# The second pair of column tiles of an input projection: eight plain products in place of seven products of a Strassen-Winograd scheme

## The chip, the cores and the metric

The kernel runs on one core of a Trainium2 chip. The metric is the device time of one execution in microseconds (us), lower is better. Engines are named as in the profile: PE is the matrix engine (PEld its weight loads), DVE the vector engine, ACT the scalar engine, POOL the GpSimd engine, SP the engine that issues most loads and stores. L85 is line 85 of the kernel before.

## What is computed

One step of a decoder layer for 1024 prompt rows and 64 sample rows, all in float32:

```python
h = rmsnorm(x, g_pre)
proj = h @ w_in                       # 1024 x 6656
p_in, p_gate, c_val, c_glu, c_gate, q, x_gate = slices of 512 columns
merge_logits = the other 3 x 1024 columns
a     = pool_mix(p_in) * silu(p_gate)
u     = c_val * sigmoid(c_glu)        # then a causal depthwise conv, width 31, layernorm, silu
bconv = cv * silu(c_gate)
cattn = attention(q, mem_kv(memory)) * silu(x_gate)
merged = sum_n sigmoid(merge_logits[n]) * (branch_n @ w_branch[n])
x_new = x + rmsnorm(merged @ w_out, g_post)
```

Outputs are x_new, the last rows of the two mixers' inputs, and the memory keys and values.

## The kernel before

**Products.** Each float32 operand is split into two float16 parts, high and low (`hilo`: ACT writes the high part, L75, and DVE the low one, L77 or L79; some low parts with no scale go to POOL). A product of two split operands takes three matmuls (`mm3`, L85, L88, L89); below, "a product" is one such matmul of 128 x 128 weights with 512 columns.

**Pairs.** The projection's columns are worked through in pairs of 128-column tiles. A pair's weights are a 2 x 2 block: a11, a12 (first tile, upper and lower 512 rows of the weight) and a21, a22 (second tile). The tokens are a 2 x 2 block too: B11, B21 (first 512 tokens, upper and lower features) and b12, B22 (second 512). `pair` makes the four result blocks with the seven products of Strassen-Winograd, 7 x 12 matmuls, from sums s1 to s4 of weight blocks and T1 to T4 of token blocks. s1 to s4 are made by ACT negating two blocks (L498) and four accumulating DMAs on POOL's queue (L499, L505 to L507). The T's are made once, in `startup`, and split into the big tile BO.

The first pair (sigmoid of c_glu, channels 0 to 255) is worked in `startup` by eight plain products, 8 x 12 matmuls (`first`): two tiles, two token halves, two feature halves. The second pair (c_val, `val_pair(0)`) is the first that goes through `pair`; its loads and two of its seven products are drawn into `startup` (`early`). Then follow the pairs of q, x_gate, and so on: 25 pairs after the first.

**Samples.** The 64 sample rows take 64-column matmuls in stage m5 of each pair (`mm_smp`), from a11, a12, a22 and a21. For these a21 is split (L75 on ACT, L79 on DVE), in `base0` or `prep5`.

**Order.** The stage loop at the file's end emits, for each stage, the loads 12 stages ahead, the weight sums 8 ahead, the splits 3 ahead, then the stage's matmuls, its evaluation, and a number of convolution taps and of side-job steps given by RATES. Side jobs are generators: `states` (the sample states), `mem_kv` (memory keys and values), attention heads, pooling, layer norm. A scheduler then reorders the emitted instructions on each engine; on the chip each engine runs its list in that order. Convolution taps (L712, L714) keep their program order.

**Startup.** x is loaded, its row norms found, the first 512 tokens turned by PE transposes (`flip`, L228), scaled and split (B11, B21). `second_half(k)` does the same for the second 512 tokens, feature tiles k and k+4: DVE L292 and L295 make the differences `tq` from which the T's come, and L79 splits b12, B22 and T1. T3 and T4 are two POOL subtractions for each k (L312, L313) and two splits.

Of the kernel before, what the change touches and what calls it, by code (L numbers as in the profile page):

```python
# [7 lines left out]
F32 = mybir.dt.float32  # L8
# [30 lines left out]
RATES = [(1.1, 2.2), (1, 1.4), (0.9, 1), (1, 1.2), (2.3, 1.4), (1.1, 1.8), (0.8, 0.9), (1.3, 0.2), (0.8, 1)]  # L39
# [7 lines left out]
def hybrid_layer_kernel(ctx, tc, i, o):  # L47
# [167 lines left out]
    BS = cst.tile([P, 2, KT, NS], F16, name="BS")  # L215
    g_pre = cst.tile([P, KT], F32, name="g_pre")
# [19 lines left out]
    def startup():  # L236
# [34 lines left out]
        xs_r = rstds([xs])  # L271
        mem["r"] = rstds(mems)
# [9 lines left out]
        first(0, 0, [lambda k: bo(B11, k), lambda k: bo(B21, k)])  # L282
# [7 lines left out]
        def second_half(k):  # L290
# [6 lines left out]
            hilo(tq[k][:, 0], *bo(T1, k), -1.0)  # L297

        second_half(0)
        yield  # L300
        first(1, 0, [lambda k: bo(B11, k), lambda k: bo(B21, k)])
        yield
        for k in range(1, 4):
            second_half(k)
            yield
        for k in range(4):
            hilo(tq[k][:, 1], *bo(T2, k), -1.0)
        for r in range(2):
            first(r, HALF, [lambda k: (b12[k // 2][:, 0, k % 2], b12[k // 2][:, 1, k % 2]), lambda k: bo(B22, k)])
            for k in (2 * r, 2 * r + 1):  # L310
                t3, t4 = half(), half()
                nc.gpsimd.tensor_tensor(t3, tq[k][:, 1], hx[k][:, 0], ALU.subtract)  # L312
                nc.gpsimd.tensor_tensor(t4, hx[k][:, 1], tq[k][:, 1], ALU.subtract)  # L313
# [12 lines left out]
            hilo(hs_, BS[:, 0].rearrange("p k n -> p (k n)"), BS[:, 1].rearrange("p k n -> p (k n)"))  # L326
# [9 lines left out]
    def mem_kv():  # L336
        memT = [Q([P, 2, KT // 2, NMEM], F16) for _ in range(2)]
# [103 lines left out]
    def mm_smp(out, w, kh, start, stop):  # L441
        mm3(out, [(w[:, 0, k, :], w[:, 1, k, :], BS[:, 0, 4 * kh + k, :], BS[:, 1, 4 * kh + k, :]) for k in range(4)], start, stop)

    early = {}

    def pair(c0, dest, block, smp, sc=1.0 / WS):


        v = {}
# [44 lines left out]
        def base0():  # L494
            spl("a21", lambda: A(1, 0))
# [75 lines left out]
        ahead = not stages  # L571
# [4 lines left out]
        if ahead:  # L576
            early.update(
                load=[*loads], first=lambda: (prep_a11(), m0(), e0()),
                second=lambda: (prep3(), m3()))
# [753 lines left out]
    for _ in start:  # L1333
        pass
# [68 lines left out]
```

## Time and profile before

| what | value |
|---|---|
| runs | 1017.92, 934.6, 937.97 us; median 937.97 |
| the profiled execution | 935.87 us, of which the span from first to last instruction is 933.8 us |
| mean granted PE clock | 0.97 |
| PE busy | 858.4 us (92%), 5765 matmuls |
| DVE busy | 741.3 us (79%), 1141 instructions |
| ACT, POOL busy | 452.8 us (48%), 359.3 us (38%) |
| memory traffic | read 62.37 MB, written 6.33 MB |

How to read it: a row of the timeline is "start, duration, engine, line, operation, out<-in, shape, xcount [idle time of the engine just before <- what ended it]". A row of the windows is "from:to length, then busy time and (xcount) of PE, PEld, DVE, ACT, POOL, then the granted PE clock, the share of the DMA engines in use and GB/s". Matmuls overlap in the pipeline: their start-to-start distance is their price, and a duration of 0.38 us is longer than that.

### The profile page before, as it was taken

What the parts mean: (1) busy time and instruction counts of PE and PEld (TensorE: products, weight loads), DVE (VectorE), ACT (ScalarE), POOL (GpSimd) and SP (SyncE); (2) the same over time, 40 slices, a digit from 0 to 9 for tenths busy, and PEclk for the clock granted to TensorE, in tenths of its full rate; (3) what the DMA queues carried; (4) which work ended last, traced back from release to release, by engine and by line L of the source; (5) the groups of instructions that cost most, each with busy time, mean ns of one, the idle gap of its engine ahead of it and who ended that gap; (6) DMA issues with size and microseconds to landing.
All of it is one profiled execution on the core that took longest, in us unless ns stands there. A gap on an engine that the chain in (4) does not pass through costs nothing.

```text
span 933.8 us, 15219 instructions
## 1 busy us (share of the span) xinstructions
PE 858.4 (92%) x5765; PEld 459.7 (49%) x5765; DVE 741.3 (79%) x1141; ACT 452.8 (48%) x964; POOL 359.3 (38%) x384
## 2 busy tenths in 40 slices
PE   5869999899999869999989989999999999968996
PEld 3325444554455435555444545555545555535532
DVE  4698599999968999999999696559565544699876
ACT  7767446564653613323345444346445443545542
POOL 1364152344243380311235664516364213285500
PEclk8889999999999988999999999999999999998998
DMA  8635742225556222334444345545554656310132
GB/s 296 160 62 157 205 107 57 58 68 136 126 191 159 91 39 79 70 79 93 97 97 102 73 102 116 121 97 105 123 122 101 138 131 216 85 57 24 69 124 90
DMA packets 99238, 103.23 MB, mean 111 GB/s; under 512 B 5231, under 2 KB 71781, under 8 KB 99149
## 3 DMA queue, kind: packets, MB, share of 16 engines
q1 hardware_dynamic: 82748, 68.24, 23.3%
q0 software_dynamic: 16416, 34.02, 20.4%
q8 instruction: 45, 0.74, 0.3%
q14 instruction: 29, 0.23, 0.1%
HBM read 62.37 MB, written 6.33 MB: 74 GB/s over the span
## 4 chain that ended last, share of the span: by engine, by line
PE 40%; DVE 20%; issue 3%; DMA 2%; ACT 1%; POOL 0%; DVEq 0%; ACTq 0%; POOLq 0%
PE pm L85 10%; PE pm L88 9%; PE pm L89 9%; DVE q L714 6%; PE pb L88 4%; PE pb L89 3%; PE pb L85 3%; DVE ws L79 3%; DVE ws L77 2%; DMA raw<-raw 2%; DVE BO L79 1%; DVE q L1151 1%; DVE q L466 1%; DVE q L1090 1%; DVE q L1082 1%
## 5 line engine op out<-in xcount | busy, mean ns | idle before, releaser
L85 PE MATMUL pm<-BO,ws 128*128 128x512 f16 x836 | 320.7, 385 | 18.6 <-DVE q L787 4.8
L88 PE MATMUL pm<-BO,ws 128*128 128x512 f16 x836 | 321.2, 384 | 2.2 <-DVE BO L79 1.6
L89 PE MATMUL pm<-BO,ws 128*128 128x512 f16 x836 | 320.3, 384 | 1.2 <-DVE ws L77 0.9
L79 DVE SCALAR_TENSOR_TENSOR ws<-raw,ws 128x512 f16<-128x512 f32 x228 | 194.2, 869 | 60.1 <-ACT ws L75 58.5
L88 PEld LDWEIGHTS <-ws 128*128 128x128 f16 x1548 | 149.1, 99 | 135.4 <-issue 29.9
L85 PEld LDWEIGHTS <-ws 128*128 128x128 f16 x1548 | 148.8, 99 | 126.1 <-issue 17.2
L89 PEld LDWEIGHTS <-ws 128*128 128x128 f16 x1548 | 149.2, 99 | 123.5 <-issue 8.2
L75 ACT ACTIVATE ws<-raw 128x512 f16<-128x512 f32 x228 | 138.1, 625 | 121.8 <-PE pm L89 50.4
L714 DVE SCALAR_TENSOR_TENSOR q<-q,cw,q 128x1024 f32<-128x1024 f32 x120 | 174.2, 1462 | 0.2
L85 PE MATMUL pb<-q,ws 128*128 128x364 f16 (+1 forms) x288 | 92.2, 323 | 13.2 <-ACT q L75 8.4
L88 PE MATMUL pb<-q,ws 128*128 128x364 f16 (+1 forms) x288 | 92.5, 321 | 0.0
L89 PE MATMUL pb<-q,ws 128*128 128x364 f16 (+1 forms) x288 | 92.3, 321 | 0.0
L499 POOL DMA_DIRECT2D raw<-raw x25 | 21.9, 876 | 157.6 <-ACT raw L498 133.3
L513 ACT ACTIVATE h<-pm 128x512 f32<-128x512 f32 x75 | 44.2, 590 | 63.5 <-PE pm L89 63.3
L1151 DVE SCALAR_TENSOR_TENSOR q<-pb,q 128x364 f32<-128x364 f32 (+1 forms) x72 | 37.2, 527 | 22.1 <-PE pb L89 20.4
L466 DVE SCALAR_TENSOR_TENSOR q<-pm,h 128x512 f32<-128x512 f32 x51 | 34.8, 683 | 23.1 <-PE pm L89 13.2
L75 ACT ACTIVATE q<-q 128x1024 f16<-128x1024 f32 (+2 forms) x37 | 35.7, 972 | 29.6 <-DVE q L863 15.5
L507 POOL DMA_DIRECT2D raw<-raw x25 | 23.4, 935 | 66.3 <-issue 16.8
L506 POOL DMA_DIRECT2D raw<-raw x25 | 21.7, 867 | 65.6 <-DMA raw<-raw 25.3
L77 POOL TENSOR_TENSOR q<-q,q 128x1024 f16<-128x1024 f32 (+1 forms) x17 | 32.5, 1921 | 30.2 <-ACT q L75 30.2
L498 ACT ACTIVATE raw<-raw 128x512 f32<-128x512 f32 x50 | 30.9, 625 | 26.4 <-DVE ws L79 26.2
L85 PE MATMUL pm<-BS,ws 128*128 128x64 f16 x416 | 43.7, 194 | 0.0
(242 smaller groups left out, 1311.9 us busy)
## 6 DMA issues: line engine op xcount, KB each, us to landing
raw<-in_w_in SPq DMA_DIRECT2D x104, 256.0 KB, 3.0
raw<-raw POOLq DMA_DIRECT2D x100, 256.0 KB, 3.2
q<-in_x_prompt SPq DMA_DIRECT2D x16, 512.0 KB, 9.4
q<-q POOLq DMA_DIRECT2D x14, 544.0 KB, 5.8
raw<-in_w_branch SPq DMA_DIRECT2D x24, 256.0 KB, 3.8
q<-in_w_mem_kv SPq DMA_DIRECT2D x8, 512.0 KB, 6.8
q<-in_cache_mem_k SPq DMA_DIRECT2D x8, 512.0 KB, 3.7
q<-in_cache_mem_v SPq DMA_DIRECT2D x8, 512.0 KB, 9.4
```

The costliest lines, as they stand in the source:

```text
L75: nc.scalar.activation(hi, src, AF.Copy, scale=scale)
L77: (eng or nc.vector).tensor_tensor(lo, src, hi, ALU.subtract)
L79: nc.vector.scalar_tensor_tensor(lo, src, scale, hi, ALU.mult, ALU.subtract)
L85: ins = nc.tensor.matmul(out, wh, xh, start=start and j == 0, stop=False, skip_group_check=partial)
L88: nc.tensor.matmul(out, wh, xl, start=False, stop=False, skip_group_check=partial)
L89: nc.tensor.matmul(out, wl, xh, start=False, stop=stop and j == n - 1, skip_group_check=partial)
L466: nc.vector.scalar_tensor_tensor(dst, ps, sc, base, ALU.mult, ALU.add)
L498: nc.scalar.activation(A(1, kh), A(1, kh), AF.Copy, scale=-1.0)
L507: nc.gpsimd.dma_start(out=A(0, 1), in_=A(0, 0), accum_op=ALU.add)
L513: nc.scalar.activation(v[name], ps, AF.Copy, scale=sc)
L714: ins = nc.vector.scalar_tensor_tensor(acc, src, wj, acc, ALU.mult, ALU.add)
L1151: nc.vector.scalar_tensor_tensor(g, p, 1.0 / WS, g, ALU.mult, ALU.mult)
```

## The change

* The pair of c_val, channels 0 and 1 (`val_pair(0)`), is made by the new `plain_pair`: eight plain products (8 x 12 matmuls) instead of seven. Its four weight blocks are split in `startup` and no sums are made of them. The four products of the first token half are emitted ahead of most of `second_half`, and the remaining four are the pair's own first two stages; its samples are a third. A pair now stands for three stages at the head of the stage list instead of seven, and RATES gives each of them 4.8 side-job steps instead of 2.2.
* In every other pair, the second tile's samples are made from a22 and s1 instead of a22 and a21: the operand of s1 is the negated upper half of the samples (BSN), that of a22 the difference of the halves (BSD). s1 is minus the sum of a21 and a22, so the result is the same block. Both operands are split once, in `startup`. a21 is not split any more: one ACT and one DVE instruction of 128 x 512 less in each of 24 pairs. With the four splits that `plain_pair` doesn't need, 28 splits go on each of the two engines (228 to 200). POOL's queue loses four accumulating DMAs and three multiplications with the seven-product form of that pair.
* The splits of T1 are emitted after the second half's first product, those of T2, T3 and T4 after both.
* The loads of the states and of the memory are emitted in `startup`, after `second_half`, as the first step of their generators; the row norm of the samples goes behind them and that of the memory into `mem_kv`.

Core of the diff:

```diff
@@
-RATES = [(1.1, 2.2), (1, 1.4), (0.9, 1), (1, 1.2), (2.3, 1.4), (1.1, 1.8), (0.8, 0.9), (1.3, 0.2), (0.8, 1)]
+RATES = [(1.1, 4.8), (1, 1.4), (0.9, 1), (1, 1.2), (2.3, 1.4), (1.1, 1.8), (0.8, 0.9), (1.3, 0.2), (0.8, 1)]
@@
-        xs_r = rstds([xs])
-        mem["r"] = rstds(mems)
@@
-        first(0, 0, [lambda k: bo(B11, k), lambda k: bo(B21, k)])
+        first(0, 0, early["ops", 0])
@@
             hilo(p, *bo(B22, k), gk)
-            hilo(tq[k][:, 0], *bo(T1, k), -1.0)
@@
         second_half(0)
-        yield
-        first(1, 0, [lambda k: bo(B11, k), lambda k: bo(B21, k)])
-        yield
-        for k in range(1, 4):
-            second_half(k)
-            yield
-        for k in range(4):
-            hilo(tq[k][:, 1], *bo(T2, k), -1.0)
+        first(1, 0, early["ops", 0])
+        early["split"](0)
+        second_half(1)
+        early["first"](0)
+        early["split"](1)
+        second_half(2)
+        early["first"](1)
+        second_half(3)
+        for j in (states(), mem_kv()):
+            next(j)
+            jobs.append(j)
+        xs_r = rstds([xs])
         for r in range(2):
-            first(r, HALF, [lambda k: (b12[k // 2][:, 0, k % 2], b12[k // 2][:, 1, k % 2]), lambda k: bo(B22, k)])
-            for k in (2 * r, 2 * r + 1):
-                t3, t4 = half(), half()
-                nc.gpsimd.tensor_tensor(t3, tq[k][:, 1], hx[k][:, 0], ALU.subtract)
-                nc.gpsimd.tensor_tensor(t4, hx[k][:, 1], tq[k][:, 1], ALU.subtract)
-                hilo(t3, *bo(T3, k))
-                hilo(t4, *bo(T4, k), eng=nc.gpsimd)
+            first(r, HALF, early["ops", HALF])
             if r:
                 break
+            for k in range(4):
+                hilo(tq[k][:, 0], *bo(T1, k), -1.0)
...
+            hilo(hs_[:, :n], flat(BSN[:, 0]), flat(BSN[:, 1]), -1.0)
+            hd = half()[:, :n]
+            nc.vector.tensor_tensor(hd, hs_[:, n:], hs_[:, :n], ALU.subtract)
+            hilo(hd, flat(BSD[:, 0]), flat(BSD[:, 1]))
+        for k in range(4):
+            hilo(tq[k][:, 1], *bo(T2, k), -1.0)
+        for k in range(4):
+            t3, t4 = half(), half()
+            nc.gpsimd.tensor_tensor(t3, tq[k][:, 1], hx[k][:, 0], ALU.subtract)
+            nc.gpsimd.tensor_tensor(t4, hx[k][:, 1], tq[k][:, 1], ALU.subtract)
+            hilo(t3, *bo(T3, k))
+            hilo(t4, *bo(T4, k), eng=nc.gpsimd)
@@
+    def plain_pair(c0, block, smp):
+        raw, w = {}, {}
...
+        def split(r):
+            for kh in range(2):
+                w[r, kh] = new_ws()
+                hilo(raw[kh][:, r], w[r, kh][:, 0], w[r, kh][:, 1], WS)
+        def prod(r, t0):
+            p = pm()
+            for kh in range(2):
+                x = w[r, kh], early["ops", t0][kh]
+                mm3(p, [(x[0][:, 0, k, :], x[0][:, 1, k, :], *x[1](k)) for k in range(4)], kh == 0, kh == 1)
+            block(r, t0, p, 1.0 / WS)
...
+        early.update(load=[ldw(0), ldw(1)], split=split, first=lambda r: prod(r, 0))
+        for f in (lambda: prod(0, HALF), lambda: prod(1, HALF), samples):
+            stages.append([[], None, f, None, [], *rate, None])
@@
             spl("a22", lambda: A(1, 1))
-            spl("a21", lambda: A(1, 0))
@@
-            spl("a21", lambda: A(1, 0))
             spl("a22", lambda: A(1, 1))
@@
-            mm_smp(v["s"][:, NS : 2 * NS], v["w", "a22"], 1, True, False)
-            mm_smp(v["s"][:, NS : 2 * NS], v["w", "a21"], 0, False, True)
+            mm_smp(v["s"][:, NS : 2 * NS], v["w", "a22"], BSD, True, False)
+            mm_smp(v["s"][:, NS : 2 * NS], v["w", "s1"], BSN, False, True)
```

The scheduler gives every engine another order over about the first half of its list; after that the order is nearly the same, and the last eighth is as before on each. Three places, first as it was and then as it is. Lines are each version's own: L292, L295 are now L293, L296; L466 is L520, L712 to L729 are L757 to L774, L951 is L996, L1151 is L1196.

**DVE, the second token half in `startup`.** q_328 to q_331 before, and q_300 to q_303 now, are `tq` of k = 0 to 3; pb_332, pb_340 and pb_304, pb_312 are the PSUM banks of the turned tokens; q_326 and q_298 take b12.

```order
L292 SCALAR_TENSOR_TENSOR q_328<-pb_332,g_pre,q_136 128x512
L145 RECIPROCAL t_283<-t_279 128x2
L295 SCALAR_TENSOR_TENSOR q_328<-pb_340,g_pre,q_328 128x512
L150 TENSOR_TENSOR t_285<-t_283 128x2
L79 SCALAR_TENSOR_TENSOR q_326<-pb_332,g_pre,q_326 128x512
L151 TENSOR_TENSOR t_285<-t_285,t_281 128x2
L79 SCALAR_TENSOR_TENSOR BO<-q_328,BO 128x512
L152 TENSOR_SCALAR t_285<-t_285 128x2
L292 SCALAR_TENSOR_TENSOR q_329<-pb_394,g_pre,q_137 128x512
```

```order
L293 SCALAR_TENSOR_TENSOR q_300<-pb_304,g_pre,q_134 128x512
L296 SCALAR_TENSOR_TENSOR q_300<-pb_312,g_pre,q_300 128x512
L79 SCALAR_TENSOR_TENSOR q_298<-pb_304,g_pre,q_298 128x512
L79 SCALAR_TENSOR_TENSOR BO<-q_300,BO 128x512
L79 SCALAR_TENSOR_TENSOR ws_770<-raw_667,ws_770 128x512
L293 SCALAR_TENSOR_TENSOR q_301<-pb_352,g_pre,q_135 128x512
L79 SCALAR_TENSOR_TENSOR ws_881<-raw_688,ws_881 128x512
L79 SCALAR_TENSOR_TENSOR BO<-pb_312,g_pre,BO 128x512
```

The memory's row norm (t_279 to t_285) has left this place, and two weight splits of the q and x_gate pairs (ws_770, ws_881) stand in it. From the first scaling of the first token half (L264, now L265) to the last split of B22, the DVE list has 52 instructions of 128 x 512 and 4 of 128 x 1024 before, 51 and 2 now. The split `BO<-q` of T1 still stands inside, although it is emitted later.

**SP, the loads after the start.** raw_642, raw_645 before and raw_664, raw_667 now are the weights of the q pair; raw_724, raw_727 and raw_685, raw_688 those of the x_gate pair; raw_1104 is the pair after. A `raw` tile has four buffers.

```order
L195 DMA raw_642<-in_w_in 128x4x128 x2
L195 DMA raw_645<-in_w_in 128x4x128 x2
L405 DMA q_672<-in_state_conv 120x2x512
L408 DMA q_674<-in_state_pool 120x512
L410 DMA q_676<-in_pool_w 128x4x128
L195 DMA raw_724<-in_w_in 128x4x128 x2
L195 DMA raw_727<-in_w_in 128x4x128 x2
L344 DMA q_815<-in_w_mem_kv 128x2x512
```

```order
L196 DMA raw_664<-in_w_in 128x4x128 x2
L196 DMA raw_667<-in_w_in 128x4x128 x2
L196 DMA raw_685<-in_w_in 128x4x128 x2
L196 DMA raw_688<-in_w_in 128x4x128 x2
L422 DMA q_462<-in_state_conv 120x2x512
L425 DMA q_464<-in_state_pool 120x512
L427 DMA q_466<-in_pool_w 128x4x128
L166 DMA q_468<-in_mem_prompt 128x1024
L166 DMA q_470<-in_mem_prompt 128x1024
L196 DMA raw_1104<-in_w_in 128x4x128 x2
L361 DMA q_857<-in_w_mem_kv 128x2x512
```

The memory's rows (q_468, q_470), which stood right behind the sample rows, have moved to behind the states, and the first memory weights (q_815, now q_857) stand behind the first two loads of one pair more than before.

**DVE, at the end of the sample attention.** sxs is the attention's result for the samples, on which the last products of the first merge stages wait; q_3601 (now q_3575) and q_2565 (now q_2610) are convolution accumulators.

```order
L712 TENSOR_SCALAR q_3601<-q_2806,cw,parT 128x1024
L728 TENSOR_REDUCE v_3559<-q_3532 128x32
L728 TENSOR_REDUCE v_3605<-q_3562 128x32
L714 SCALAR_TENSOR_TENSOR q_3601<-q_2806,cw,q_3601 128x1024
L729 TENSOR_SCALAR q_1045<-v_3559,parT 128x32
L951 TENSOR_TENSOR sxs<-pb_2621,sxs 128x256
L729 TENSOR_SCALAR q_1045<-v_3605,parT 128x32
```

```order
L759 SCALAR_TENSOR_TENSOR q_2610<-q_443,cw,q_2610 128x1024
L773 TENSOR_REDUCE v_3530<-q_3486 128x32
L79 SCALAR_TENSOR_TENSOR ws_3804<-raw_3648,ws_3804 128x512
L773 TENSOR_REDUCE v_3559<-q_3533 128x32
L1196 SCALAR_TENSOR_TENSOR q_3232<-pb_3514,q_3232 128x364
L759 SCALAR_TENSOR_TENSOR q_2610<-q_443,cw,q_2610 128x1024
L996 TENSOR_TENSOR sxs<-pb_2568,sxs 128x256
L774 TENSOR_SCALAR q_1034<-v_3530,parT 128x32
```

sxs now stands ahead of the first tap L757 and of both L774, and behind two taps, one weight split and one evaluation.

More of the change, by code (lines that the diff above doesn't have):

```diff
@@ L215, in hybrid_layer_kernel @@
     BS = cst.tile([P, 2, KT, NS], F16, name="BS")
+    BSN = cst.tile([P, 2, KT // 2, NS], F16, name="BSN")
+    BSD = cst.tile([P, 2, KT // 2, NS], F16, name="BSD")
     g_pre = cst.tile([P, KT], F32, name="g_pre")
@@ L280, in first @@
             nc.scalar.activation(sg0[r][:, t0 : t0 + HALF], p, AF.Sigmoid, scale=1.0 / WS)
-        first(0, 0, [lambda k: bo(B11, k), lambda k: bo(B21, k)])
+        early["ops", 0] = [lambda k: bo(B11, k), lambda k: bo(B21, k)]
+        early["ops", HALF] = [lambda k: (b12[k // 2][:, 0, k % 2], b12[k // 2][:, 1, k % 2]), lambda k: bo(B22, k)]
+        first(0, 0, early["ops", 0])
         scale_x(xt[4:6], rs_[0], True)
@@ L336, in mem_kv @@
     def mem_kv():
+        mems = [load(i["mem_prompt"][0, t * P : (t + 1) * P, :], P) for t in range(2)]
+        yield
+        mem["r"] = rstds(mems, Q([P, D]))
         memT = [Q([P, 2, KT // 2, NMEM], F16) for _ in range(2)]
@@ L439, in mm_op, with mm_smp, ldw, f @@
         mm3(out, [(w[:, 0, k, :], w[:, 1, k, :], BO[:, n, 0, k, :], BO[:, n, 1, k, :]) for k in range(4)], start, stop, True, pinned)
-    def mm_smp(out, w, kh, start, stop):
-        mm3(out, [(w[:, 0, k, :], w[:, 1, k, :], BS[:, 0, 4 * kh + k, :], BS[:, 1, 4 * kh + k, :]) for k in range(4)], start, stop)
+    def mm_smp(out, w, x, start, stop):
+        mm3(out, [(w[:, 0, k, :], w[:, 1, k, :], x[:, 0, k, :], x[:, 1, k, :]) for k in range(4)], start, stop)
+    BS0, BS1 = BS[:, :, : KT // 2], BS[:, :, KT // 2 :]
     early = {}
+    def plain_pair(c0, block, smp):
+        raw, w = {}, {}
+        def ldw(kh):
+            def f():
+                raw[kh] = load_pair(kh, c0)
+            return f
+        def split(r):
[8 more added lines that the diff above has]
+            block(r, t0, p, 1.0 / WS)
+        def samples():
+            p = pm()
+            for r in range(2):
+                for kh, x in enumerate((BS0, BS1)):
+                    mm_smp(p[:, r * NS : (r + 1) * NS], w[r, kh], x, kh == 0, kh == 1)
+            for r in range(2):
+                smp(r, p[:, r * NS : (r + 1) * NS])
+        early.update(load=[ldw(0), ldw(1)], split=split, first=lambda r: prod(r, 0))
+        for f in (lambda: prod(0, HALF), lambda: prod(1, HALF), samples):
+            stages.append([[], None, f, None, [], *rate, None])
     def pair(c0, dest, block, smp, sc=1.0 / WS):
+        if not stages:
+            plain_pair(c0, block, smp)
+            return
         v = {}
@@ L471, in prep0 @@
         def prep0():
-            if not ahead:
-                prep_a11()
+            prep_a11()
         def prep1():
@@ L575, in pair @@
         loads = [ldw(0), ldw(1)]
[L576 to L579, printed above, removed]
-            loads, preps[3], mms[0], evs[0], mms[3] = [], None, None, None, None
         for j in range(7):
@@ L1323, in hybrid_layer_kernel @@
         stages[at + s][4].append(load_x(*tts))
-    start = startup()
     for f in early["load"]:
         f()
-    next(start)
-    next(start)
-    early["first"]()
-    next(start)
-    early["second"]()
-    for _ in start:
-        pass
+    startup()
     pps = pb()
```

18 lines of the change are left out of this document (8 added, 10 removed).

## Prediction

> **What bounds the kernel now.** I read the page's busy times first, then PE's windows, then the rows where PE waits.
>
> ```profile
> PE 858.4 (92%) x5765; PEld 459.7 (49%) x5765; DVE 741.3 (79%) x1141; ACT 452.8 (48%) x964; POOL 359.3 (38%) x384
> ```
>
> ```profile
> 0.00:40.00 40.00, 29.12 (x126) 16.23 (x127) 23.53 (x56) 28.55 (x53) 9.61 (x42) 0.87 0.79 251
> 40.00:70.00 30.00, 17.69 (x72) 7.62 (x71) 27.30 (x37) 21.86 (x36) 17.36 (x15) 0.83 0.35 68
> 70.00:130.00 60.00, 60.00 (x424) 31.97 (x422) 45.28 (x60) 35.29 (x67) 19.20 (x20) 1.00 0.57 160
> 130.00:310.00 180.00, 171.14 (x1250) 96.42 (x1249) 160.49 (x246) 97.75 (x216) 69.26 (x66) 1.00 0.44 110
> 310.00:355.00 45.00, 32.54 (x257) 17.89 (x255) 43.51 (x40) 16.10 (x32) 24.28 (x12) 0.85 0.26 67
> 355.00:450.00 95.00, 94.68 (x619) 51.47 (x617) 95.00 (x116) 34.27 (x64) 15.62 (x17) 1.00 0.39 86
> 450.00:560.00 110.00, 100.96 (x669) 50.01 (x667) 98.06 (x111) 50.23 (x99) 59.87 (x51) 0.98 0.41 93
> 560.00:815.00 255.00, 253.92 (x1714) 138.69 (x1713) 149.76 (x242) 118.26 (x231) 98.53 (x97) 1.00 0.54 124
> 815.00:850.00 35.00, 25.03 (x147) 12.96 (x146) 33.33 (x49) 15.97 (x45) 25.34 (x25) 0.90 0.17 53
> ```
>
> PE is the bound nearly everywhere: it is busy without a break from 70 to 130, from 355 to 450 and from 560 to 815 us. There a DVE instruction less is worth nothing, although DVE is full from 355 to 450. Time lies open where PE idles: in the startup (40 to 70: 12 us idle, at a clock of 0.83), at 310 to 355 (12 us, clock 0.85), at 450 to 560 (9 us) and in the tail, whose order the change leaves alone.
>
> The hole in the startup, on PE:
>
> ```profile
> 22.41 0.59 PE L88 MATMUL pm<-BO,ws 128*128 128x512 f16 x1 [0.63 <-DVE BO L77]
> 30.04 0.38 PE L88 MATMUL pm<-BO,ws 128*128 128x512 f16 x1
> 30.25 0.38 PE L89 MATMUL pm<-BO,ws 128*128 128x512 f16 x1
> 40.62 0.38 PE L89 MATMUL pm<-BO,ws 128*128 128x512 f16 x1
> 44.96 0.59 PE L85 MATMUL pm<-q,ws 128*128 128x512 f16 x1 [3.96 <-ACT q L75]
> 47.15 0.63 PE L89 MATMUL pm<-q,ws 128*128 128x512 f16 x1
> 47.57 0.63 PE L85 MATMUL pm<-q,ws 128*128 128x512 f16 x1
> 50.81 1.09 PE L228 MATMUL pb<-ident,q 128*128 128x128 f32 x4 [1.75 <-DVE BO L79]
> 58.80 0.59 PE L85 MATMUL pm<-q,ws 128*128 128x512 f16 x2 [2.03 <-ACT q L75]
> ```
>
> ```profile
> 41.00:68.00 27.00, 14.69 (x59) 6.32 (x58) 24.30 (x33) 19.13 (x33) 15.36 (x13) 0.81 0.35 68
> ```
>
> A product costs 0.21 us at full clock (30.04 to 30.25) and 0.42 at the clock granted after a wait (47.15 to 47.57). In 27 us PE runs 59 matmuls, at most 59 x 0.21 = 12.4 us of work. DVE is busy for 24.3 of these 27 us: it makes the splits of the second token half, which PE waits for directly or behind ACT. So the hole is DVE's.
>
> **The change part by part.**
>
> *Startup.* PE now has 24 + 24 products of the second pair that need the first token half alone, so it has work while DVE prepares the second half. What decides is when DVE finishes the last split of B22, because behind it PE has all operands of both pairs. These rows bound the run of DVE that leads there:
>
> ```profile
> 15.24 1.41 DVE L264 SCALAR_TENSOR_TENSOR q<-pb,g_pre,h 128x512 f32<-128x512 f32 x2 [0.57 <-ACT h L257]
> 71.42 0.74 DVE L79 SCALAR_TENSOR_TENSOR BO<-pb,g_pre,BO 128x512 f16<-128x512 f32 x1
> ```
>
> ```profile
> 15.00:72.00 57.00, 49.72 (x74) 0.82 0.51 126
> ```
>
> ```profile
> 46.28 3.01 DVE L152 TENSOR_SCALAR t<-t 128x2 f32<-128x2 f32 x1
> 54.38 0.74 DVE L79 SCALAR_TENSOR_TENSOR q<-pb,g_pre,q 128x512 f16<-128x512 f32 x1
> 55.04 2.32 DVE L79 SCALAR_TENSOR_TENSOR BO<-q,BO 128x512 f16<-128x512 f32 x1
> ```
>
> ```profile
> L312 POOL TENSOR_TENSOR h<-q,q 128x512 f32<-128x512 f32 x4 | 5.7, 1435 | 0.2
> L77 POOL TENSOR_TENSOR BO<-q,BO 128x512 f16<-128x512 f32 x4 | 5.7, 1442 | 18.7 <-ACT BO L75 18.7
> L77 POOL TENSOR_TENSOR BO<-h,BO 128x512 f16<-128x512 f32 x3 | 4.8, 1598 | 3.0 <-ACT BO L75 3.0
> L313 POOL TENSOR_TENSOR h<-q,q 128x512 f32<-128x512 f32 x3 | 4.6, 1528 | 0.6 <-DVE BO L77 0.6
> ```
>
>
> Before, it runs from 15.2 to 72.1: 52 instructions of 128 x 512, 4 of 128 x 1024 and 18 small ones. At their undisturbed 0.64 us each from start to start (0.66 from 54.38 to 55.04), 0.7 and 0.15 these would take 33.3 + 2.8 + 2.7 = 39 us. It was busy 49.7, so some 11 us are instructions that last longer than they need, such as 2.32 for a split of 0.7 or 3.01 for a tiny one, beside POOL's work; and 57 - 49.7 = 7 us are idle.
>
> Now the list has 51, 2 and 14: 32.6 + 1.4 + 2.1 = 36 us. That is hardly less, so the gain is mostly in what stands beside it. The last fence groups POOL's fourteen vector instructions from 19 to 71 us. Of these (four low parts of the first half, seven subtractions, three low parts of T4) eight can fall into the run: behind the first four subtractions POOL's next entry is a low part of T4, which waits for ACT's high part, and ACT has that behind all its splits of the second half. So lengthening is 8/14 of 11 = 6 us, and idle time, for weights still landing and for ACT's order, I leave at 5. DVE ends at 15.2 + 36 + 6 + 5 = 62. The ends: 51 with neither, 70 with all 18 us of both kept. By the first, PE itself would decide: to that point its list has 132 products and some 40 transposes from 22.4 us on, 132 x 0.21 = 27.7, ten at the slow clock 2.1 more, and 4 for the transposes (four take 1.09 at half clock): 57.
>
> From there PE's list holds 142 products, 96 of 64 columns and some 28 transposes until the memory keys' products end. Before, an almost equal stretch (137, 96 and 28) ran gapless:
>
> ```profile
> 68.17 0.38 PE L85 MATMUL pm<-BO,ws 128*128 128x512 f16 x1
> 103.15 0.38 PE L89 MATMUL pb<-q,q 128*128 128x512 f16 x1
> ```
>
> That is 35.2 us, so 36.3 now, ending at 98.3 instead of 103.4; and 20 products of the q pair more stand ahead of that point, worth 4.3. Startup net: 103.4 - 98.3 + 4.3 = **9.4 us won**, the 12 additional products (12 x 0.21 = 2.5) counted in. The ends: 14.4 won (PE's own 57) and 1.4 (70).
>
> *a21 never split.* 24 ACT and 24 DVE instructions less, 28 with the second pair's.
>
> ```profile
> L79 DVE SCALAR_TENSOR_TENSOR ws<-raw,ws 128x512 f16<-128x512 f32 x228 | 194.2, 869 | 60.1 <-ACT ws L75 58.5
> ```
>
> At 0.87 us that is 24 us of DVE, but most of it falls where PE is busy all the time. It pays only where DVE's list holds PE up:
>
> ```profile
> 335.76 4.34 DVE L712 TENSOR_SCALAR q<-q,cw,parT 128x1024 f32<-128x1024 f32 x1
> 343.41 5.00 DVE L729 TENSOR_SCALAR q<-v,parT 128x32 f32<-128x32 f32 x1
> 348.33 0.41 DVE L951 TENSOR_TENSOR sxs<-pb,sxs 128x256 f32<-128x256 f32 x1
> 349.08 0.76 PE L85 MATMUL pb<-q,ws 128*128 128x360 f16 x2 [8.36 <-ACT q L75]
> ```
>
> PE waits 8.4 us for the sample attention's result, which DVE reaches behind a tap of 4.34 us (L712) and a tiny L729 of 5.00. In the new order both stand behind it; one tap, one split and one evaluation more stand ahead, about 2.3 us. That would be 7 us; but most of the 9.3 is waiting beside POOL, which may hit another instruction as well. I take **4 won**, bounds 0 and 7. In 450 to 560 and in 130 to 310 PE idles 9 us each; two or three splits less there may win 2 or a new order lose 3: I take 0.
>
> *At nothing.* The sample operands BSN and BSD (three DVE, two ACT instructions, under 2 us) stand behind B22's last split, under PE's gapless stretch; without that cover they would cost their 2 us. Sample matmuls keep their number. s1's weights are now held until stage m5, a21's no longer: no more of the 13 buffers. The moved loads of states and memory rows are wanted only in that stretch too. Four accumulating DMAs less free POOL's queue while PE doesn't wait for them.
>
> *Sum.* 933.8 - 9.4 - 4 = 920.4 of span; with the 2.1 us by which the execution (935.87) exceeds its span 922.5. The median of the runs, 937.97, is 2.1 above that execution, so I say **923 us**.
>
> **A rule that speaks against it.** On the row of 2.32 us above bears what the Trainium skill says in "SBUF — State Buffer", section "SBUF: two separate sides": DVE and GpSimd share one port pair as an exclusive lock, and a DVE instruction with two SBUF inputs waits out a GpSimd instruction that reads SBUF. The trace agrees here: the split with one PSUM input took 0.74. By this rule the seven T splits `BO<-q` that still stand ahead of B22's last split can each be blocked, which would give rival 1.
>
> **The rivals.**
>
> 1. *The hole moves instead of closing.* Seven T splits stay in DVE's run; if POOL's work lengthens them as it did the one of 2.32 us, and the idle time stays, DVE ends at 70. Startup then wins 1.4, and nothing at 349: 935.9 - 1.4 = 934.5. For it: nearly equal counts, 52 and 51. Against it: POOL's list stops behind four subtractions.
>
> 2. *The memory's weights come late: slower.* Place: the first memory product on PE.
>
> ```profile
> 81.55 2.19 SPq L344 DMA_DIRECT2D q<-in_w_mem_kv  x4
> 92.15 0.59 PE L85 MATMUL pb<-q,q 128*128 128x512 f16 x2
> ```
>
> It starts 10.6 us after the load is issued. Now PE gets to it at about 62 + 25 = 87, so the load must be issued by 76; but on SP it stands behind raw_1104, which needs a buffer whose last split is DVE's 26th instruction behind B22's, some 14 us later, that is at 76, if the memory rows' norm, which also stands ahead there, isn't late. Each us after 76 is one of PE's. From 76 + 9.4 + 4 = 89 on, the kernel is slower; at 100 it would take 935.9 + 11 = 947. Against it: nothing ahead of that split waits for PE.
>
> 3. *The wait at 349 goes entirely, and DVE's relief also shortens 450 to 560*: startup 12, 7 there, 3 later: 935.9 - 22 = 914.
>
> 4. *It doesn't do what it says*: PE idles in the second half for want of ACT (40 to 70: 21.9 us busy of 30). The last split then comes no sooner than in rival 1, with the same time.
>
> **How the numbers follow.** A change of 2% (18.8 us, to 919.2) is about what a measurement of this kernel can tell. Chances: the forecast, 917 to 931, 0.6; rivals 1 and 4 together 0.2; rival 2 0.08; rival 3 0.12. The unknown costs give 935.9 - 14.4 - 9 = 912.5 to 935.9 - 1.4 + 3 = 937.5, and so the range is 912 to 938; it leaves out some 0.06 of rival 3 and 0.08 of rival 2. Faster by over 2%: rival 3 and a third of the lower half of the forecast, 0.22; slower by over 2%: half of rival 2, 0.04; within: 0.74.
>
> **What would show it.** Right: from 41 to 68 us PE's window holds over 100 matmuls instead of 59, at a clock above 0.9; DVE's last split `BO<-pb` ends near 62; the memory keys' products end near 98; the gap before the products on sxs is about 4 us instead of 8.4; `ws<-raw` on DVE is there 200 times; from 560 us on, shifted, the windows are as before. Wrong: a last split near 70; a gap of some us before the first memory product; or a startup that comes early and a loss of the same size at 130 to 310, where DVE is busy for 160 of 180 us.

## The result, and the profile after

The changed kernel takes 939.16 us (median of 17 runs), the one before, in 17 runs beside it, 934.60: a ratio of 1.0055, 95% interval 1.0041 to 1.0068. That is slower by half a per cent, where 923 was forecast. One run of each seventeen was far longer (1783.55 and 1017.92 us) and is left out of the ratio. The base was a little off too: the 935.87 us of the profiled execution, from which the forecast took its terms, is 1.3 us above the median of the seventeen.

The profiled execution took 941.47 us, its span 939.7. The page's busy times, and then five windows:

```profile
PE 860.9 (92%) x5777; PEld 460.6 (49%) x5777; DVE 722.8 (77%) x1116; ACT 433.4 (46%) x933; POOL 353.1 (38%) x377
```

```profile
41.00:68.00 27.00, 22.94 (x127) 11.42 (x126) 25.06 (x36) 17.64 (x32) 13.89 (x14) 0.87 0.48 110
70.00:130.00 60.00, 53.38 (x361) 28.67 (x360) 37.06 (x50) 29.65 (x56) 11.61 (x14) 0.94 0.52 143
130.00:310.00 180.00, 168.56 (x1201) 93.95 (x1200) 155.43 (x234) 92.17 (x209) 68.92 (x65) 0.98 0.42 109
310.00:355.00 45.00, 31.92 (x285) 18.15 (x281) 44.09 (x35) 17.97 (x34) 28.57 (x14) 0.91 0.25 60
355.00:450.00 95.00, 92.43 (x602) 50.04 (x600) 94.46 (x118) 32.31 (x62) 15.30 (x16) 0.97 0.37 84
```

The hole did close: 127 matmuls from 41 to 68 us where there were 59. But from 70 to 130 PE, gapless before, runs 361 instead of 424 at a clock of 0.94. What happened there stands in one row each of PE, ScalarE and SP:

```profile
87.22 1.12 PE L370 MATMUL pb<-ident,q 128*128 128x128 f32 x4 [5.99 <-ACT es L439]
107.19 0.38 PE L89 MATMUL pb<-q,q 128*128 128x512 f16 x1
```

```profile
74.75 1.17 ACT L433 ACTIVATE us<-pb 128x240 f32<-128x240 f32 x4
84.67 0.63 ACT L549 ACTIVATE raw<-raw 128x512 f32<-128x512 f32 x1 [8.75 <-DMA raw<-in_w_in]
85.20 0.82 ACT L75 ACTIVATE q<-pb,parT 128x256 f16<-128x256 f32 x2
86.21 0.47 ACT L75 ACTIVATE q<-pb,parT 128x256 f16<-128x256 f32 x1 [0.19 <-DVE q L79]
86.58 0.58 ACT L439 ACTIVATE es<-pb 128x480 f32<-128x480 f32 x1
```

```profile
80.58 0.93 SPq L196 DMA_DIRECT2D raw<-in_w_in  x2
81.61 0.96 SPq L361 DMA_DIRECT2D q<-in_w_mem_kv  x2
```

Read from below. SP issues the weights of the second attention pair (raw_1104) at 80.58, because only then is a raw buffer free. ScalarE's next entry is the sign change of exactly these weights (L549, in `base0`), and it waits 8.75 us for them. Behind it stand the splits of the turned memory rows and es, small instructions whose operands PE had made by 80.3 us, and PE waits for these: 5.99 us. From 80 to 90 us its granted clock is 0.72. The memory keys' products end at 107.6; before, at 103.5. VectorE waits for the same splits, 5.15 us until 85.69.

Why the buffer was free at 80.6 and not at 76, as the prediction had it, shows on VectorE:

```profile
58.02 0.73 DVE L79 SCALAR_TENSOR_TENSOR BO<-pb,g_pre,BO 128x512 f16<-128x512 f32 x1
69.35 1.20 DVE L151 TENSOR_TENSOR t<-t,t 128x2 f32<-128x2 f32 x1
72.94 2.28 DVE L356 TENSOR_SCALAR q<-q,t 128x1024 f32<-128x1024 f32 x2
78.14 2.40 DVE L79 SCALAR_TENSOR_TENSOR ws<-raw,ws 128x512 f16<-128x512 f32 x2
```

The last split of B22 ends at 58.8, not 72.2 (62 was forecast). The 26 instructions behind it then take 22 us instead of the 14 counted. In between stands the memory rows' norm, with five instructions on 2 elements of 1.0 to 1.2 us each (the sixth takes 0.15).

The second term of the sum, sxs, on VectorE, GpSimd and PE:

```profile
343.86 9.55 DVE L759 SCALAR_TENSOR_TENSOR q<-q,cw,q 128x1024 f32<-128x1024 f32 x1
353.33 0.41 DVE L996 TENSOR_TENSOR sxs<-pb,sxs 128x256 f32<-128x256 f32 x1
```

```profile
342.95 0.86 POOL L558 DMA_DIRECT2D raw<-raw  x1 [2.87 <-DVE ws L79]
343.52 8.80 POOL L770 TENSOR_TENSOR q<-us,cw 128x992 f32<-128x992 f32 x4
```

```profile
354.09 0.76 PE L85 MATMUL pb<-q,ws 128*128 128x360 f16 x2 [7.12 <-ACT q L75]
```

The tap that now stands right ahead of sxs takes 9.55 us where it needs 1.27. It begins 0.3 us after a train (several instructions of one engine, back to back) of four products of the convolution's samples on GpSimd, and ends 1.1 us after these are through, about its own running time. PE waits 7.12 us instead of 8.36, not 4.

### The profile page after: what moved, and what is told of

It is laid out like the page before. It is cut to its first block, busy times and chain, and to the rows that moved or that the text cites. A ratio compares the mean times of both kernels' runs of the same rounds, so it can differ in the third digit from the quotient of the medians.

```text
span 939.7 us, 15132 instructions
## 1 busy us (share of the span) xinstructions
PE 860.9 (92%) x5777; PEld 460.6 (49%) x5777; DVE 722.8 (77%) x1116; ACT 433.4 (46%) x933; POOL 353.1 (38%) x377
## 4 chain that ended last, share of the span: by engine, by line
PE 43%; DVE 31%; DMA 9%; issue 8%; ACT 6%; POOL 2%; SPq 1%; DVEq 0%; ACTq 0%; POOLq 0%
DVE q L759 12%; PE pm L85 10%; PE pm L88 10%; PE pm L89 10%; DVE ws L79 5%; DMA raw<-in_w_in 5%; PE pb L88 4%; PE pb L89 4%; PE pb L85 4%; DVE ws L77 3%; DVE BO L79 2%; DMA raw<-raw 1%; ACT ws L75 1%; DMA q<-q 1%; DVE q L1196 1%
## 5 line engine op out<-in xcount | busy, mean ns | idle before, releaser
L79 DVE SCALAR_TENSOR_TENSOR ws<-raw,ws 128x512 f16<-128x512 f32 x200 | 168.6, 861 | 41.6 <-ACT ws L75 40.5
L759 DVE SCALAR_TENSOR_TENSOR q<-q,cw,q 128x1024 f32<-128x1024 f32 x120 | 181.0, 1519 | 0.4
L75 ACT ACTIVATE ws<-raw 128x512 f16<-128x512 f32 x200 | 118.4, 624 | 87.7 <-PE pb L89 29.2
L549 ACT ACTIVATE raw<-raw 128x512 f32<-128x512 f32 x48 | 30.2, 628 | 85.7 <-DMA raw<-in_w_in 57.7
L550 POOL DMA_DIRECT2D raw<-raw x24 | 21.8, 907 | 126.8 <-ACT raw L549 120.1
L1196 DVE SCALAR_TENSOR_TENSOR q<-pb,q 128x364 f32<-128x364 f32 (+1 forms) x72 | 37.2, 528 | 26.1 <-PE pb L89 20.9
L520 DVE SCALAR_TENSOR_TENSOR q<-pm,h 128x512 f32<-128x512 f32 x48 | 32.7, 683 | 27.9 <-PE pm L89 18.2
L557 POOL DMA_DIRECT2D raw<-raw x24 | 20.8, 866 | 87.9 <-DVE ws L79 29.3
L77 POOL TENSOR_TENSOR q<-q,q 128x1024 f16<-128x1024 f32 (+1 forms) x17 | 35.4, 2088 | 39.8 <-ACT q L75 39.5
L558 POOL DMA_DIRECT2D raw<-raw x24 | 20.8, 866 | 73.3 <-DVE ws L79 43.5
L709 ACT ACTIVATE q<-q 128x512 f32<-128x512 f32 x36 | 22.6, 629 | 39.0 <-DVE q L520 38.7
```

The costliest lines, as they stand in the source:

```text
L75: nc.scalar.activation(hi, src, AF.Copy, scale=scale)
L77: (eng or nc.vector).tensor_tensor(lo, src, hi, ALU.subtract)
L79: nc.vector.scalar_tensor_tensor(lo, src, scale, hi, ALU.mult, ALU.subtract)
L520: nc.vector.scalar_tensor_tensor(dst, ps, sc, base, ALU.mult, ALU.add)
L549: nc.scalar.activation(A(1, kh), A(1, kh), AF.Copy, scale=-1.0)
L709: nc.scalar.activation(dst, src, AF.Sigmoid, scale=scale)
```

## The experiments

Theory A, from these rows: the startup's gain is lost to ScalarE's queue, and what the unsplit a21 should bring is eaten by VectorE waiting beside GpSimd. Rival B: whatever the startup wins is given back later, because VectorE is nearly full from 130 to 500 us. Each recorded expectation below names its own two theories, which are not always these. All runs in one table, of twelve executions each (the first two of seventeen, e10 five, e11 four); the ratio is to the kernel before, run beside each, with its 95% interval; the times of events are from one profiled execution of each.

| run | median us | ratio | keys' products end | sxs starts | last tap starts |
|---|---|---|---|---|---|
| before | 934.60 | 1 | 103.5 | 348.3 | 498.7 |
| changed | 939.16 | 1.0055 (1.0041 to 1.0068) | 107.6 | 353.3 | 497.0 |
| e4_pin | 932.65 | 0.9991 (0.9966 to 1.0016) | 100.5 | 343.5 | 489.4 |
| e5_mem_early | 935.43 | 1.0018 (0.9994 to 1.0042) | 100.5 | 343.0 | 487.2 |
| e2_a21_alone | 937.73 | 1.0046 (1.0020 to 1.0071) | 101.5 | 350.8 | 493.6 |
| e3_plain_alone | 932.08 | 0.9984 (0.9965 to 1.0003) | 98.5 | 341.1 | 496.0 |
| e6_pin_cdve | 928.76 | 0.9952 (0.9935 to 0.9969) | 100.9 | 324.7 | 482.7 |
| e7_plain_cdve | 932.06 | 0.9984 (0.9966 to 1.0002) | 97.6 | 326.8 | 494.8 |
| e8_before_cdve | 932.05 | 0.9980 (0.9964 to 0.9997) | 102.3 | 333.1 | 496.9 |
| e9_a21_cdve | 930.62 | 0.9964 (0.9947 to 0.9981) | 103.4 | 335.0 | 493.7 |
| e12_after_cdve | 935.67 | 1.0025 (1.0009 to 1.0041) | 105.9 | 331.4 | 489.2 |
| e10_before_half | 928.92 | 0.9958 (0.9940 to 0.9976) | 104.2 | 335.5 | (60 taps) |
| e11_plain_half | 907.83 | 0.9724 (0.9707 to 0.9742) | 98.8 | 322.2 | (60 taps) |
| e13_all | 927.58 | 0.9937 (0.9918 to 0.9956) | 101.8 | 329.4 | 486.7 |

**The sign change behind the memory's splits.** To the changed kernel:

```
-                nc.scalar.activation(A(1, kh), A(1, kh), AF.Copy, scale=-1.0)
+                ins = nc.scalar.activation(A(1, kh), A(1, kh), AF.Copy, scale=-1.0)
+                if c0 == 5 * W + 2 * P:
+                    tc.keep_in_program_order(ins)
```

> The changed kernel with one thing more: the sign change of the second attention pair's weights (L549, the instruction on which ScalarE waited 8.75 us for its load at 84.67) is kept in program order, so that it stands behind the memory's splits on ScalarE. Theory A (the queue head on ScalarE costs the startup's gain): the gap of 5.99 us before the turning of the memory projection at 87.22 shrinks below 2 us, the clock of 0.72 in 80 to 90 us goes, and 5 to 8 us of it reach the end: 931 to 934 us, a ratio to the kernel before of 0.992 to 0.999. Theory B (what the startup wins is given back anyway in the stretch where VectorE is nearly full, 130 to 400 us): the gap goes, but the time stays within 2 us of the changed kernel, 937 to 940, a ratio of 1.003 to 1.007.

PE and ScalarE in this run:

```profile
81.59 0.66 PE L370 MATMUL pb<-ident,q 128*128 128x128 f32 x4 [0.68 <-ACT es L439]
```

```profile
80.96 0.58 ACT L439 ACTIVATE es<-pb 128x480 f32<-128x480 f32 x1
82.13 1.16 ACT L75 ACTIVATE ws<-raw 128x512 f16<-128x512 f32 x2
92.82 0.61 ACT L549 ACTIVATE raw<-raw 128x512 f32<-128x512 f32 x1
```

In the traces the lists of all other engines are, entry by entry, those of the changed kernel, and on ScalarE this one entry has moved behind 16 others. The gap falls from 5.99 to 0.68 us, although the loads are issued about as late as in the changed kernel (raw at 80.18, the memory's weights at 81.21). 932.65 us lies in theory A's range; the ratio falls by 1.0055 - 0.9991 = 0.0064, which is 6.0 us. So the place of one instruction in ScalarE's list costs all by which the change is slower, and a little more. Rival B is right about the rest: PE is 3.0 us ahead of the kernel before at the keys' products, with 32 products more behind it (272 against 240, the 12 additional ones among them), some 7 us in all, and of this lead only 0.8 us (0.0009 x 934), within the interval, are left at the end. The long tap ahead of sxs is no part of what the pin removed, for it stands here too, beside the same train:

```profile
334.02 9.55 DVE L761 SCALAR_TENSOR_TENSOR q<-q,cw,q 128x1024 f32<-128x1024 f32 x1
```

**The memory rows' load and norm early again.** The two loads stand ahead of `par`, and `mem["r"] = rstds(mems)` ahead of `early["ops", 0]`, as in the kernel before.

```
+    mems = [load(i["mem_prompt"][0, t * P : (t + 1) * P, :], P) for t in range(2)]
     par = half((P, P))
...
+        mem["r"] = rstds(mems)
         sg0.update({r: Q([P, T]) for r in range(2)})
...
     def mem_kv():
-        mems = [load(i["mem_prompt"][0, t * P : (t + 1) * P, :], P) for t in range(2)]
         yield
-        mem["r"] = rstds(mems, Q([P, D]))
```

> The changed kernel with the memory rows loaded early again (ahead of the parameter rows) and their norm made in the startup, ahead of the first pair's first products, as in the kernel before; the eight plain products and the unsplit a21 stay. Theory A (the norm's tiny VectorE instructions beside GpSimd's subtractions, behind rows that land late, hold up the weight splits, through them the raw buffer, the load and ScalarE's queue): VectorE is 5 to 7 us earlier at the split that frees the raw buffer (78 to 80 us in the changed kernel), the wait of 8.75 us on ScalarE shrinks to 2 to 4, and the time falls by 3 to 6 us, 933 to 936 us. Theory B (given back later anyway): 937 to 940 us. A third outcome, the norm takes its time from the splits of the second token half instead, and the hole at 41 to 68 us opens again by 3 to 5 us: 939 to 943 us.

The time falls as theory A said, and the wait on ScalarE is 2.67 us. Its reason was wrong: SP's load is issued at 79.45, only 1.1 us sooner. What changed is ScalarE's list, in which four of the memory's splits now stand ahead of the sign change. That the norm's place costs anything of its own is not shown: the interval overlaps with the pin's.

**One half of the change each.** The unsplit a21 on the kernel before, and the plain products with a21 split again:

```
-            mm_smp(v["s"][:, NS : 2 * NS], v["w", "a22"], 1, True, False)
-            mm_smp(v["s"][:, NS : 2 * NS], v["w", "a21"], 0, False, True)
+            mm_smp(v["s"][:, NS : 2 * NS], v["w", "a22"], BSD, True, False)
+            mm_smp(v["s"][:, NS : 2 * NS], v["w", "s1"], BSN, False, True)
...
-            spl("a21", lambda: A(1, 0))
```

> The kernel before with the second half of the change alone: the sample products from a22 with the halves' difference and from s1 with minus the first half, a21 never split in any pair (28 ScalarE and 28 VectorE instructions fewer, five small ones more); the second pair stays as it was. Theory A (the loss sits in the startup's order): this part is worth 0 to 4 us, 931 to 936 us, ratio 0.995 to 1.000. Theory B (the order that the scheduler makes of the fewer splits costs the middle, 260 to 410 us, its gaps): 1 to 4 us slower, 937 to 940 us, ratio 1.001 to 1.004.

> The changed kernel with a21 split again and the sample products from a22 and a21 as in the kernel before: the eight plain products and the new startup alone. Theory A (the loss sits in the startup's order, and the unsplit a21 is worth little): the gap near 81 to 87 us is still there, and the time is 938 to 944 us, ratio 1.003 to 1.010. Theory B (the loss is from the order in the middle that comes with the unsplit a21): 931 to 936 us, ratio 0.995 to 1.001.

For both, theory B's range came out. a21 alone (203 weight splits instead of 228) is slower by 4.3 us (0.0046 x 934); the plain products alone are not slower, and without a stall: with a21 split again SP issues the first memory weights at 60.99 and the next pair's weights behind them, at 81.67, no sign change waits for a load, and the keys' products end at 98.5, where 98.3 had been worked out for the whole change. So the stall needs both halves, and a21 has a cost of its own. Where it may come from is seen on VectorE and GpSimd of the run with a21 alone:

```profile
319.88 0.68 DVE L476 SCALAR_TENSOR_TENSOR q<-pm,h 128x512 f32<-128x512 f32 x1
320.49 12.14 DVE L722 SCALAR_TENSOR_TENSOR q<-q,cw,q 128x1024 f32<-128x1024 f32 x1
332.55 0.52 DVE L1159 SCALAR_TENSOR_TENSOR q<-pb,q 128x364 f32<-128x364 f32 x1
```

```profile
320.76 4.53 POOL L77 TENSOR_TENSOR q<-q,q 128x1024 f16<-128x1024 f32 x2
324.94 4.52 POOL L733 TENSOR_TENSOR q<-us,cw 128x992 f32<-128x992 f32 x2
329.11 2.43 POOL L77 TENSOR_TENSOR q<-q,q 128x1024 f16<-128x1024 f32 x1
```

One tap lasts 12.14 us instead of 1.27, while five GpSimd instructions run back to back. PE is not behind at once: by 355 us it has started 2122 matmuls, the kernel before 2121. Later a tap of 5.52 at 386.75 puts the evaluations behind it back, and PE waits:

```profile
398.76 0.38 PE L85 MATMUL pm<-BO,ws 128*128 128x512 f16 x1 [3.55 <-DVE q L476]
```

By 450 us it has started 2709 against 2738, so the loss falls between 355 and 450. Which part of it is the long taps, and which the new order of the lists, is not separated.

**The convolution's sample products on VectorE.** If this waiting is the cost, it should go when GpSimd's products leave that stretch. One word changes, in the pinned kernel, the plain one, the kernel before, the one with a21 alone and the changed one without the pin. The scheduler then reorders a part of the lists (in the pinned kernel 1008 of VectorE's 1116 entries keep their order):

```
-            nc.gpsimd.tensor_tensor(pr, src, cw[:, ch, :].unsqueeze(1).unsqueeze(1).to_broadcast([P, 4, DS, CW]), ALU.mult)
+            nc.vector.tensor_tensor(pr, src, cw[:, ch, :].unsqueeze(1).unsqueeze(1).to_broadcast([P, 4, DS, CW]), ALU.mult)
```

> The changed kernel with the pinned sign change (as in the run before) and with the sixteen products of the convolution's samples (L770, 128x992, on GpSimd 2.45 to 3.1 us each) on VectorE instead, where a reduction over the same 992 elements takes 1.17. Theory A (VectorE's instructions wait out trains of these products: the tap of 9.55 us that ends where the sample attention's result sxs begins, and one of 4.90 at 383): VectorE gets 16 x 1.2 = 19 us of work and is rid of some 20 to 25 us of waiting, no VectorE instruction between 310 and 400 us lasts over 4 us, sxs comes at 338 to 341 instead of 343.5, and the time falls by 2 to 5 us, 928 to 931 us. Theory B (it is VectorE's own list, not the waiting beside GpSimd, that holds sxs and the evaluations): the additional 19 us cost 2 to 8 us, 935 to 941 us.

> The eight plain products alone (a21 split again), with the sixteen products of the convolution's samples on VectorE instead of GpSimd. In the run without this the taps at 335.20 (5.96 us) and 349.04 (5.51 us) waited beside them. Theory A (waiting beside GpSimd): 926 to 930 us, against 932.1 without it. Theory B (VectorE's own list): 934 to 940 us.

> The kernel before with the sixteen products of the convolution's samples on VectorE instead of GpSimd. There a tap of 4.34, an evaluation of 5.00 and a split of 4.40 us waited beside them. Theory A (waiting beside GpSimd): 2 to 5 us faster, 929 to 932 us; the startup's gain of the eight plain products then shows as 2 to 6 us between this kernel and the plain one with the same move. Theory B (VectorE's own list): 936 to 942 us.

> The kernel before with a21 never split and the convolution's sample products on VectorE. a21 alone was 4 us slower than the kernel before; the move alone brought that kernel to 932.05. Theory A (the 28 splits fewer shorten VectorE's list by 17 us, and what they gave was eaten by a tap that waited 12.14 us for a train of GpSimd's products): with the train gone the unsplit a21 is a gain of 2 to 5 us, 927 to 930 us. Theory B (the loss comes from the new order of the lists whatever GpSimd does): 934 to 938 us.

> The changed kernel, its sign change not pinned, with the convolution's sample products on VectorE. With the pin this measured 928.76 us. Theory A (the stall on ScalarE at 81 to 87 us leaves VectorE, too, without work for some 6 us, and VectorE's list sets the time to 500 us): 933 to 937 us. Theory B (the stall only moves PE, which gets it back where it waits for VectorE anyway): 928 to 931 us.

There are eight such products, not sixteen. In the changed kernel on GpSimd, and in the pinned one on VectorE:

```profile
L770 POOL TENSOR_TENSOR q<-us,cw 128x992 f32<-128x992 f32 x8 | 20.1, 2649 | 0.0
```

```profile
L772 DVE TENSOR_TENSOR q<-us,cw 128x992 f32<-128x992 f32 x8 | 10.6, 1366 | 0.0
```

```profile
324.69 0.42 DVE L998 TENSOR_TENSOR sxs<-pb,sxs 128x256 f32<-128x256 f32 x1
```

The same window of the pinned kernel, without the move and with it:

```profile
310.00:355.00 45.00, 33.65 (x289) 19.21 (x290) 44.89 (x42) 13.31 (x26) 23.35 (x12) 0.89 0.18 39
310.00:355.00 45.00, 42.34 (x351) 24.84 (x352) 44.87 (x56) 15.77 (x31) 7.02 (x5) 0.96 0.22 50
```

From 310 to 355 us VectorE does 56 instructions instead of 42 in the same 44.9 busy us, and PE 351 instead of 289. Four of the five kernels became faster, as theory A has it and near its ranges: before by 0.0020 (1.9 us), changed by 0.0030, pinned by 0.0039, a21 alone by 0.0082 (7.7 us). The changed one, with its stall, stays 0.0073 (6.8 us) above the pinned one, and again the two differ in the place of that one entry alone, so the stall costs about the same in both settings. The plain kernel did not move (0.9984 both times), against both theories: its sxs came 14 us sooner, and its last tap 1 us. The 2 to 6 us that were expected between it and the kernel before with the same move did not come either (932.06 and 932.05). And a21, which alone cost 0.0046, with GpSimd's products gone brings 0.0016 on the kernel before and, between the plain and the pinned kernel, 0.0032 (the intervals of both comparisons overlap). That a21's loss is the waiting beside GpSimd fits this, since the kernel with the longest tap gains most by the move. It is not shown: the plain kernel, with taps of 5.96 and 5.51 us, gained nothing, and the move also changed the order. A gain of a21 without the trains is too small to call shown.

**Half the taps.** In two kernels the odd taps are left out, 60 of the 120 that accumulate, so the convolution is incomplete and VectorE has an estimated 72 us (60 x 1.2) less to do:

```
         def f():
+            if j % 2:
+                return
             if j == 0:
```

> The kernel before with every second tap of the convolution left out (60 of 120 taps L714, 1.2 us each; the convolution is then wrong): 72 us less on VectorE between 130 and 500 us. It is the base for the next run. By theory A (VectorE's list, full without a break from 355 to 500 us, sets when PE gets on there) the time falls by 15 to 30 us, to 904 to 919; by theory B (PE's products set it, as the prediction had it) it falls by no more than the gaps at 310 to 355 and 450 to 560 that wait for VectorE, 8 to 15 us: 919 to 926.

> The eight plain products alone (a21 split again) with the same 60 taps left out. With all taps this kernel led the one before by 11 us at 100 us and by 2 us at the end. Theory A (the lead is handed back because PE then waits for VectorE's full list): with VectorE relieved the lead stays, this run is 8 to 12 us below the kernel before with half the taps. Theory B (the lead is lost for another reason, such as PE's own additional products or the tail): again 0 to 4 us below it.

The windows of the kernel before, of before with half the taps, and of the plain kernel with half the taps:

```profile
355.00:500.00 145.00, 138.78 (x899) 72.82 (x897) 145.00 (x170) 54.83 (x104) 37.76 (x36) 0.99 0.39 87
```

```profile
130.00:310.00 180.00, 172.41 (x1265) 97.96 (x1264) 148.81 (x230) 98.25 (x220) 65.47 (x66) 1.00 0.45 114
355.00:450.00 95.00, 91.34 (x596) 48.66 (x594) 74.86 (x95) 34.43 (x64) 18.32 (x22) 0.98 0.37 83
```

```profile
130.00:310.00 180.00, 177.64 (x1391) 103.44 (x1390) 142.45 (x235) 106.93 (x232) 71.31 (x68) 1.00 0.45 117
355.00:450.00 95.00, 90.85 (x592) 47.41 (x590) 66.41 (x85) 35.61 (x69) 23.31 (x26) 0.97 0.39 87
```

VectorE of the kernel before has not one free microsecond from 355 to 500. With half the taps it has 20 to 29 of 95, and now the plain products are worth 928.92 - 907.83 = 21.1 us, against 1.5 (0.0016 x 934) with all taps.

The traces show where the lead goes. Count the columns of all matmuls that PE has started, 512 to a product, and take off the 12 additional products. With all taps the plain kernel leads the one before by 10.1 us at 130, by 8.1 at 355 and by 1.7 at 450. In that last stretch its PE, unlike that of the kernel before, waits for VectorE's evaluations, and VectorE is no further: by 450 it has begun 548 of its 1137 instructions, in the kernel before 549 of 1141. The plain kernel's window and one of these waits:

```profile
355.00:450.00 95.00, 89.96 (x591) 48.44 (x591) 95.00 (x117) 33.99 (x65) 16.19 (x17) 0.98 0.36 84
```

```profile
357.29 0.38 PE L85 MATMUL pm<-BO,ws 128*128 128x512 f16 x1 [2.80 <-DVE q L513]
```

With half the taps the lead is 10.6, 13.0 and 11.6 us at the same three times. So the lead was lost to VectorE's full list, as rival B has it. Both absolute forecasts missed: before with half the taps gained 4 to 5 us only (0.0042 x 934 = 3.9 by the ratio; in its place PE then waits for ScalarE's evaluations, 3.66 us at 383 and 4.07 at 464), and 21 is more than that lead; 130 to 310 runs freer as well, in a new order of the list. How much of the 21 is that order stays open.

**Pin, move and early norm together.** The last run joins the three edits:

> The changed kernel with three things more: the sign change pinned, the convolution's sample products on VectorE, and the memory rows' load and norm early, as in the kernel before. Theory A (what VectorE has done by 130 us sets the time): the norm's tiny instructions no longer stand beside GpSimd's subtractions, VectorE has done 1 to 3 instructions more by 130 us (153 with the pin and the move), and the time is 925 to 928 us against 928.8 without the early norm. Theory B (once the sign change is pinned, nothing in the startup waits for the norm): 928 to 931 us.

It measured 927.58 us, in theory A's range, but VectorE had done 150 instructions by 130 us, not more than 153, and the interval overlaps with that of the pin and the move alone. Nothing is shown for the norm. Both kernels are faster than the one before and the changed one.

## Why the prediction was wrong, point by point

- *The hole.* Right. 127 matmuls from 41 to 68 us, last split of B22 at 58.8 (62 forecast). Of its terms, the idle time was right (5.7 us for 5), and the lengthening beside GpSimd was too large: VectorE was busy for 38.1 us up to there, 2 and not 6 above the 36 counted. The clock of 0.87 is short of 0.9.
- *"Before, an almost equal stretch ran gapless."* This is where the first term failed. It counted PE's list from the last split to the keys' end and took for granted that the operands would be there as before. In the plain kernel they nearly are (two waits on PE, of 1.4 and 1.3 us), and the stretch ends at 98.5, so the term of 5.1 us came out. That it did so to a tenth or two is luck: the stretch began 2.8 us sooner than forecast, at 59.2, and lasted 39.3 us instead of 36.3. In the changed kernel the sign change of raw_1104 stood ahead of es on ScalarE, and the stretch ended at 107.6. The prediction follows ScalarE's list for the splits of the second half, and does not look at it here; it reads VectorE's, SP's and PE's.
- *Rival 2* had the late load behind the raw buffer, and estimated 76 for what came at 80.6, but looked for the wait at the first memory product and for the memory's weights. The pinned run has those weights as late (81.2) and no gap. The load was the right one, the queue that waits for it was the wrong one; it had a chance of 0.08.
- *a21: 4 us at 349.* Not obtained: the instructions of 4.34 and 5.00 us stood behind sxs, as the order said, but a tap ahead of it took 9.55 us, and PE waited 7.12 us instead of 4. "Which may hit another instruction as well" was the true sentence, and it was given less than half of the 7 us. The splits less (25 with a21 alone) do shorten VectorE's list, whose last tap starts 5 us sooner there, yet that kernel is 4.3 us slower.
- *"There a DVE instruction less is worth nothing, although DVE is full."* For the kernel before by itself the sentence comes near: 60 taps less brought it 3.9 us. What failed most is what the sum made of it, that a lead of PE passes through. From 355 to 450 PE was busy 94.68 us and VectorE 95.00 of 95: both were full, and a PE that comes sooner waits there for VectorE's evaluations. Of the 9.4 us for the startup, which the plain kernel obtained at 98.5 us (5.0 of time, and 24 products, 5.2 us), 1.5 reached the end.
- *"In 450 to 560 and in 130 to 310 ... I take 0"* followed from the same sentence. The list of what would show it wrong held the case, an early startup and a loss of the same size behind it, but looked for it at 130 to 310; most of it came at 355 to 450. It was the plain kernel's case, and had no rival with a chance of its own.
- *The additional 12 products*, 2.5 us, were counted rightly; nothing in the runs speaks of more.
- *The 0.74 us of the split with one PSUM input* (at 54.38) don't show that such a split runs undisturbed beside GpSimd: up to its end at 55.12 GpSimd ran no vector instruction, and its next one begins at 55.32. The evaluation at 335.32, in the last section, does.

In sum: the stall costs 6.0 to 6.8 us, a21's new order 4.3 where the stall is not, the startup's gain passes on 1.5. These do not add up to the measured 4.6 (the stall does not arise with a21 split, and in the pinned kernel a21's cost hardly shows, 0.9991 against the plain kernel's 0.9984), so no exact split between them is claimed. The stall and the lost lead are shown by the runs; why the unsplit a21 costs time by itself stays open between the waiting beside GpSimd and the new order.

## What to carry to other kernels

Where two engines are both full in a stretch, a lead that one of them brings is worth what the other gains too; count the second engine's list to the end of the stretch, with its waits, before a term is carried to the end of the kernel. When a change sends a load later, look on every engine for the first instruction that needs it, and for what stands behind that one: a small early preparation of the next stage can hold up the present one. And work that another engine does in long trains beside the full one can be cheaper on the full engine itself: here four kernels of five gained 0.2 to 0.8%, and one gained nothing.

## What was unexpected of the hardware

An instruction of VectorE with both inputs in SBUF waited not for one GpSimd instruction but for a whole train: 9.55 us beside four, 12.14 beside five (where its record even begins 0.3 us ahead of the first), 2.1 us from start to start, with no turn for VectorE between them. The Trainium skill, "SBUF — State Buffer", section "SBUF: two separate sides", has the shared port pair as an exclusive lock for a whole instruction; the traces agree on the lock, and go further, since it was not handed over between instructions. It was in other places: in the pinned kernel, at 321 and 324 us, taps of 3.04 and 3.03 us take turns with GpSimd's 3.11 and 3.12. Which of the two happens no run here explains. An evaluation that reads PSUM ran through at its 0.52 us beside such a product (in the kernel before, at 335.32, the product from 334.96 on).

The eight products cost VectorE 10.6 us and GpSimd 20.1, and four kernels of five became faster when the full engine took them over. The Trainium skill, "Perfetto Trace Analysis", section "Optimizing Scalar/DVE Operations", says that offloading between these two engines might not help, because they share a port; here having them on GpSimd did not help.
